# Sample states of a retention layer: key-value products directly behind the query-state products

## The chip, the core and the metric

The kernel runs on one core of a Trainium2 chip. The metric is device microseconds (us) of one execution. A core has engines that run side by side and meet at semaphores: PE (TensorE, matrix products; PEld is its loading of weights), DVE (VectorE), ACT (ScalarE), POOL (GpSimd) and SP (SyncE), which in this kernel issues most of the DMAs. Each engine takes its instructions in order, so one that waits holds up all behind it on the same engine.

## The reference, cut to what matters

The kernel computes one layer of a hybrid decoder for 1024 prompt tokens and for 8 sample sequences of 4 new tokens. The part that the change touches is the retention branch of the samples, with 4 heads, keys of 256 and values of 512 elements, and a state of 256x512 for each sequence and head:

```python
def retention_chunk(q, k, v, s_prev, log_g):
    ...
    intra = jnp.einsum('bhij,bjhe->bihe', scores, v)
    q_decay = jnp.exp((idx[:, None] + 1.0) * log_g[None, :])
    cross = jnp.einsum('bihd,bhde->bihe', q, s_prev) * q_decay[None, :, :, None]
    k_decay = jnp.exp((c - 1.0 - idx)[:, None] * log_g[None, :])
    s_new = (jnp.exp(c * log_g)[None, :, None, None] * s_prev
             + jnp.einsum('bjhd,bjhe->bhde', k * k_decay[None, :, :, None], v))
    return intra + cross, s_new
```

`s_prev` is read from `state_ret` and `s_new` is an output, `ret_sample`. So every state is loaded, multiplied with the queries, scaled, increased by the products of keys and values, and stored.

## The kernel before, in words

The layer is worked off in stages: latents and gates, attention of the samples over their pages, retention, attention of the prompt, and the projections back. Nearly all large products are split in a high and a low part and take three matmuls each (`mac`, L262 to L268); `gemm` (L270) does a projection of 128 columns in three thirds of 352 tokens, with 8 such triples to a third, and takes its weights from `load_w` (L253), which loads them with SP (tile `wr`, L246), rounds them on ACT (`wh`, L247) and takes the rest on DVE (`wl`, L199).

In the retention stage the loop over heads `h` stands at L1055. For each head, `prompt_chunks` goes through the eight chunks of the prompt, and `sample_state` (L965) comes behind its last chunk. Beside both run the projections for the next head (`head_in`, L1050), or, for the last head, the MLA gate projections (`gate_tiles`). The two streams are woven at L1070: each is a Python generator that yields costs, and `woven` (L115) always continues the stream that is less far along in its total cost (27.9 or 32.4 for the first, 50.3 or 31.8 for the other). So a `yield 1.2` in `sample_state` is a place where projections may come in, and its number says how many. The order of the text is then the priority with which the framework's planner orders each engine's instructions. It may depart from it where it takes an operand to be late.

`sample_state` works in four turns `n` per head (L1017), each over half of the rows `i` and half of the key dimension `m`, with four sequences `r`:

- four query-state products into `px` (L1021), 128 rows by 32 columns of the array each, at four column positions, so that they run beside one another. In turns 2 and 3 they are held in the program's order (`keep_in_program_order`, L1024);
- `yield 1.2` (L1025);
- four key-value products into `pd` (L1029), 32 rows by 128 columns each, at four row positions. They take two PSUM banks of `ac` and two of `tr`, of three each; `px` holds the third of `ac` throughout the loop. They read `kxs` and `vst`, which do not depend on the states;
- four updates of the state on DVE (L1031), which read `pd` and overwrite the state in place, and behind every second one a DMA from SP that stores the pair (L1033);
- in turns 0 and 1, two loads of the states of turn `n + 2` (L1035, `states`, L956, issued at L961). There are four buffers `st` of two states each, so such a load waits for the store of the turn two before to be done;
- `yield 2.6` (L1036).

The states of turns 0 and 1 are loaded ahead, from within `prompt_chunks` (L942 and L952).

Of the kernel before, what the change touches and what calls it, by code (L numbers as in the profile page):

```python
# [161 lines left out]
def decode_step(ctx: ExitStack, tc: tile.TileContext, A: dict, O: dict):  # L162
# [17 lines left out]
    def tr():  # L180
        return banks["pool"].tile([P, 512], F32, tag="tr", name="tr", bufs=3)

    def ac():
        return banks["pool"].tile([P, 512], F32, tag="ac", name="ac", bufs=3)
# [7 lines left out]
    def b32(ap):  # L192
        return ap.bitcast(F32)
# [10 lines left out]
    def C(name, i=0, w=None, rows=P):  # L204
        o, ww = at[name]
        w = ww if w is None else w
        return cst[:rows, o + i * w:o + (i + 1) * w]
# [619 lines left out]
    def group_norm(po, n, qd, qd2):  # L827
        st6 = small(p4, "st6", 6, 2)
        dve.bn_stats(out=st6[:n], in_=po)
        mv = small(p4, "mv", 2, 2)  # L830
        dve.bn_aggr(out=mv[:n], in_=st6[:n])
        v = small(p4, "gv", 1, 2)
        dve.tensor_scalar(v[:n], mv[:n, 1:2], qd2, EPS, op0=ALU.mult, op1=ALU.add)
        r = small(p4, "gr", 1, 2)
        pool.tensor_tensor(out=r[:n], in0=v[:n], in1=nhalf[:n], op=ALU.pow)
        s = small(p4, "gs", 1, 2)
        dve.tensor_tensor(out=s[:n], in0=r[:n], in1=qd, op=ALU.mult)
        nb = small(p4, "gb", 1, 2)
        dve.scalar_tensor_tensor(out=nb[:n], in0=mv[:n, 0:1], scalar=-1.0, in1=s[:n], op0=ALU.mult, op1=ALU.mult)  # L839
        on = p4.tile([P, DV], F32, tag="row", name="on", bufs=2)  # L840
        act.activation(on[:n], po, AF.Identity, bias=nb[:n], scale=s[:n])  # L841
        return on

    def gate_in(h, n, cols):
        g = p4.tile([P, 4, P], F32, tag="g", name="g", bufs=3)[:, :, :n]
        sp.dma_start(g, gtD[h][:, :, cols])
        return g

    def gate_out(h, on, n, cols, g):
        pt = tr()  # L850
        for f in range(4):
            pe.transpose(pt[:, f * P:f * P + n], on[:n, f * P:(f + 1) * P], ident[:n, :n])  # L852
        for f in range(4):
            dve.scalar_tensor_tensor(out=g[:, f, :], in0=pt[:, f * P:f * P + n], scalar=gnw[:, 4 * h + f:4 * h + f + 1],
                                     in1=g[:, f, :], op0=ALU.mult, op1=ALU.mult)
        sp.dma_start(goD[h][:, :, cols], g)
# [99 lines left out]
    def states(h, i, m):  # L956

        pairs = []
        for half in range(2):
            st = p4.tile([P, 2, DV], F32, tag="st", name="st", bufs=4)  # L960
            sp.dma_start(st, A["state_ret"][0].rearrange("(r i) h (m p) e -> i m h p r e", i=2, m=2)[i, m, h][:, 2 * half:2 * half + 2])  # L961
            pairs.append(st)
        return pairs

    def sample_state(h, X):  # L965

        q, k = X["qS"], X["kS"]
        g4 = float(np.exp(NS * lg[h]))
        sl = slice(SEQ, NT)
        ks = p4.tile([P, 2, 4, 4, 8], F32, tag="knh", name="ks", bufs=2)  # L970
        for m in range(2):
            pool.tensor_copy(ks[:, m], k[:, m].rearrange("p (r x) -> p r x", x=8).unsqueeze(2).to_broadcast([P, 4, 4, 8]))
        pt = tr()
        for m in range(2):
            pe.transpose(pt[:, m * P:(m + 1) * P], ks[:, m].rearrange("p r c x -> p (r c x)"), ident)
        kt = p4.tile([P, DK], F32, tag="knl", name="kt", bufs=2)
        act.activation(kt, pt[:, :DK], AF.Copy, scale=C("kdS", h, 1))
        ks = p4.tile([P, 2, 2, NR], F32, tag="knh", name="ks2", bufs=2)
        for m in range(2):
            pool.tensor_copy(ks[:, m], k[:, m].unsqueeze(1).to_broadcast([P, 2, NR]))  # L980
        qm = p4.tile([P, 2, 288], F32, tag="row", name="qm", bufs=2)
        pool.memset(qm, 0.0)
        for m in range(2):
            pool.tensor_copy(qm[:, m].rearrange("p (b x) -> p b x", x=36)[:, :, :NS], q[:, m].rearrange("p (b t) -> p b t", t=NS))
        yield 1.0
        ps = ac()
        for n in range(8):
            for part in range(2):
                pe.matmul(ps[:2 * NR], few[:, n, :], X["W"][n][part], start=n + part == 0, stop=n == 7 and part == 1)
            yield 0.45  # L990
        vs = p4.tile([2 * NR, DV], F32, tag="vnl", name="vs", bufs=2)
        act.copy(vs, ps[:2 * NR])
        pss = tr()
        for m in range(2):
            pe.matmul(pss[:2 * NR, :NR], ks[:, m].rearrange("p c x -> p (c x)"), q[:, m], start=m == 0, stop=m == 1)
        sm = p4.tile([2 * NR, NR], F32, tag="sms", name="sms", bufs=1)
        dve.tensor_tensor(out=sm, in0=pss[:2 * NR, :NR], in1=C("maskS", h, NR, 2 * NR), op=ALU.mult)
        yield 1.0
        pt = tr()
        pe.matmul(pt, turn, vs, start=True, stop=True)  # L1000
        vr, vst = (p4.tile([P, DV], F32R, tag="vnh", name=n, bufs=2) for n in ("vr", "vst"))
        dve.tensor_copy(vr, pt)
        dve.scalar_tensor_tensor(out=vst, in0=b32(vr), scalar=C("minus", 1, 1), in1=pt, op0=ALU.mult, op1=ALU.add)
        kr = p4.tile([P, DK], F32R, tag="knl", name="kr", bufs=2)
        dve.tensor_copy(kr, kt)
        dve.scalar_tensor_tensor(out=kt, in0=b32(kr), scalar=C("minus", 0, 1), in1=kt, op0=ALU.mult, op1=ALU.add)
        kxs = []
        for i in range(2):
            kxs.append(p4.tile([P, DK], F32R, tag="knh", name="kx", bufs=2))
            dve.tensor_scalar(kxs[i], kt, C("seq2", i, 1), None, op0=ALU.mult)  # L1010
        yield 1.0
        px = ac()
        g = gate_in(h, NR, sl)
        out = O["ret_sample"][0].rearrange("(r i) h (m p) e -> i m h p r e", i=2, m=2)
        turns = [(i, m) for i in range(2) for m in range(2)]
        loaded = X["st"]
        for n, (i, m) in enumerate(turns):  # L1017
            pairs = loaded.pop(0)
            st = [pairs[r // 2][:, r % 2, :] for r in range(4)]
            for r in range(4):  # L1020
                ins = pe.matmul(px[32 * r:32 * r + 32, :], qm[:, m, 32 * (2 * r + i):32 * (2 * r + i) + 32], st[r],  # L1021
                                start=n == 0, stop=n == 3, tile_position=(0, 32 * r), skip_group_check=True)
                if n > 1:
                    tc.keep_in_program_order(ins)  # L1024
            yield 1.2  # L1025
            pd = [ac(), ac(), tr(), tr()]
            for r in range(4):
                rs = slice(32 * r, 32 * r + 32)
                pe.matmul(pd[r], kxs[i][rs, m * P:(m + 1) * P], vst[rs], start=True, stop=True, tile_position=(32 * r, 0))  # L1029
            for r in range(4):  # L1030
                dve.scalar_tensor_tensor(out=st[r], in0=st[r], scalar=g4, in1=pd[r], op0=ALU.mult, op1=ALU.add)  # L1031
                if r % 2:
                    sp.dma_start(out[i, m, h][:, r - 1:r + 1], pairs[r // 2])  # L1033
            if n < 2:
                loaded.append(states(h, *turns[n + 2]))  # L1035
            yield 2.6  # L1036
        xs = p4.tile([P, DV], F32, tag="row", name="xsb", bufs=2)
        act.copy(xs, px)
        po = ac()
        pe.matmul(po[:NR], sm, vs, start=True, stop=False)  # L1040
        pe.matmul(po[:NR], C("sel"), xs, start=False, stop=True)
        on = group_norm(po[:NR], NR, C("qdS", h, 1, NR), C("qd2S", h, 1, NR))
        yield 1.0
        if h + 1 < HR:
            late.append((h, on, NR, sl, g))
        else:
            gate_out(h, on, NR, sl, g)
            yield 0.5
# [545 lines left out]
```

## Time and profile before

| What | Value |
|---|---|
| Median of 3 runs | 2188.82 us (2184.98 to 2189.14) |
| The profiled execution | 2187.65 us, of which the span of the trace is 2185.8 us |
| PE busy | 2138.7 us |
| DVE busy | 1234.5 us |
| ACT busy | 731.1 us |
| The 16 turns of `sample_state` | 911.8 to 1363.5 us of the span, in four groups, one per head |
| Query-state products (L1021) | 128 matmul records, 605 ns median |
| Key-value products (L1029) | 64 matmul records, 496 and 490 ns median |
| State updates (L1031) | 64, 680 ns median, on DVE |
| State loads within the trace (L961) | 32, 512 KB each, 4.1 us median from issue to landing |
| State stores (L1033) | 32, 512 KB each, 3.7 us median |

The 605 ns are the record of one pass of a product. Four stand beside one another in the array, and a product of plain f32 operands has two passes, so a turn's eight records take about one us. In a timeline, a row gives the start, the duration, the engine, the line and the tiles written and read; in brackets stands the idle time before, with what ended it. Matmuls overlap by design, so the distance from one start to the next tells more of the cost than the durations do.

### The profile page before, as it was taken

To read this page: it belongs to the slowest core of one execution; us is meant where nothing else is said; L and a number is where in the kernel's file an instruction comes from. 1 tells how busy PE (TensorE), PEld (TensorE's weight loads), DVE (VectorE), ACT (ScalarE), POOL (GpSimd) and SP (SyncE) were. 2 spreads that over 40 slices of the span, in tenths; PEclk is the share of its full clock that TensorE was granted. 3 is DMA by queue.
4 is the path that set the end of the run, shared out by engine and by line. 5 is a ranking of instruction groups with operands and counts; after the bars stand their busy time and mean duration, and the time that the engine had idled before them with its cause. 6 is when DMAs were issued, how large, how long until landed. Compare 5 with 4: busy or idle time off the path is not lost.

```text
span 2185.8 us, 38552 instructions
## 1 busy us (share of the span) xinstructions
PE 2138.7 (98%) x15368; PEld 1858.5 (85%) x15368; DVE 1234.5 (56%) x2776; ACT 731.1 (33%) x1537; POOL 317.4 (15%) x511
## 2 busy tenths in 40 slices
PE   8999999999999999999999999899998999999997
PEld 7997877777777898888788887788887999999997
DVE  5424564565655356656666664778676353444465
ACT  6412322333333222221222311454556342222243
POOL 2211111111110022222121220122221000000121
PEclk9999999999999999999999999999999999999999
DMA  8447666566565321532613517110112353234243
GB/s 239 136 139 263 213 218 230 177 250 216 211 231 178 112 68 49 172 116 88 208 41 121 179 52 252 51 37 12 38 51 73 130 197 98 82 96 124 78 143 115
DMA packets 264356, 299.71 MB, mean 137 GB/s; under 512 B 26544, under 2 KB 221744, under 8 KB 260080
## 3 DMA queue, kind: packets, MB, share of 16 engines
q1 hardware_dynamic: 254960, 213.36, 31.5%
q0 software_dynamic: 9216, 83.89, 10.2%
q8 instruction: 121, 1.98, 0.4%
q14 instruction: 59, 0.48, 0.1%
HBM read 233.03 MB, written 64.17 MB: 136 GB/s over the span
## 4 chain that ended last, share of the span: by engine, by line
PE 61%; issue 4%; DVE 3%; DMA 1%; ACT 1%; POOL 1%; POOLq 0%; ACTq 0%; DVEq 0%; SPq 0%
PE mm L266 15%; PE mm L267 14%; PE mm L268 14%; PE ac L266 2%; PE ac L268 2%; PE ac L267 2%; PE mm L1302 2%; PE tr L1288 1%; PE ac L1245 1%; PE sc L652 1%; PE tr L852 1%; PE x L683 1%; PE ac L874 1%; PE ac L1246 1%; PE ac L1247 1%
## 5 line engine op out<-in xcount | busy, mean ns | idle before, releaser
L266 PE MATMUL mm<-xh,wh 128*128 128x352 f32 x1344 | 458.3, 341 | 1.0 <-ACT gev L413 0.8
L267 PE MATMUL mm<-xl,wh 128*128 128x352 f32 x1344 | 436.5, 325 | 0.0
L268 PE MATMUL mm<-xh,wl 128*128 128x352 f32 x1344 | 435.5, 324 | 0.0
L266 PEld LDWEIGHTS mm<-xh,wh 128*128 128x128 f32 x1344 | 253.1, 188 | 104.2 <-issue 86.5
L267 PEld LDWEIGHTS mm<-xl,wh 128*128 128x128 f32 x1344 | 254.3, 189 | 5.0 <-issue 2.7
L268 PEld LDWEIGHTS mm<-xh,wl 128*128 128x128 f32 x1344 | 253.9, 189 | 1.5 <-issue 1.5
L199 DVE TENSOR_TENSOR wl<-wr,wh 128x512 fp32r<-128x512 f32 (+2 forms) x251 | 168.5, 683 | 133.2 <-ACT wh L247 107.0
L247 ACT CAST wh<-wr 128x512 fp32r<-128x512 f32 x216 | 129.7, 618 | 285.0 <-PE mm L267 219.9
L648 DVE STREAM_TRANSPOSE kt<-craw 128x512 f32<-128x512 f32 x256 | 160.6, 681 | 108.3 <-PE sc L652 73.1
L413 ACT ACTIVATE gev<-mm 128x352 f32<-128x352 f32 x120 | 55.6, 464 | 233.0 <-PE mm L268 151.5
L266 PE MATMUL mm<-mh,wh 128*128 128x352 f32 x384 | 124.4, 324 | 1.8 <-DVE M L1417 1.8
L268 PE MATMUL mm<-mh,wl 128*128 128x352 f32 x384 | 124.3, 324 | 0.0
L268 PE MATMUL mm<-gh,wl 128*128 128x352 f32 x384 | 124.3, 324 | 0.0
L266 PE MATMUL mm<-gh,wh 128*128 128x352 f32 x384 | 124.3, 324 | 0.0
L267 PE MATMUL mm<-ml,wh 128*128 128x352 f32 x384 | 124.2, 324 | 0.0
L267 PE MATMUL mm<-gl,wh 128*128 128x352 f32 x384 | 124.1, 323 | 0.0
L266 PE MATMUL mm<-wv,xh 128*128 128x512 f32 x256 | 103.0, 402 | 0.0
L267 PE MATMUL mm<-wv,xh 128*128 128x512 f32 x256 | 100.9, 394 | 0.0
L268 PE MATMUL mm<-wv,xl 128*128 128x512 f32 x256 | 100.7, 393 | 0.0
L841 ACT ACTIVATE on<-ac,gb,gs 128x512 f32<-128x512 f32 (+1 forms) x36 | 28.0, 778 | 208.5 <-DVE gb L839 208.2
L652 PE MATMUL sc<-kt,q 32*32 32x512 f32 x2560 | 91.5, 600 | 0.0
L1523 POOL TENSOR_TENSOR xr<-x1h,x1l 128x352 f32<-128x352 f32 x24 | 24.4, 1039 | 406.2 <-DVE pT L199 326.1
(384 smaller groups left out, 4563.0 us busy)
## 6 DMA issues: line engine op xcount, KB each, us to landing
wr<-in_w_in_dram SPq DMA_DIRECT2D x144, 256.0 KB, 3.0
st<-in_state_ret_dram SPq DMA_DIRECT2D x32, 512.0 KB, 4.1
out_ret_sample_dram<-st SPq DMA_DIRECT2D x32, 512.0 KB, 3.7
wr<-in_w_ple_gate_dram SPq DMA_DIRECT2D x48, 256.0 KB, 2.7
gt<-gev SPq DMA_DIRECT2D x48, 176.0 KB, 1.8
gl<-go SPq DMA_DIRECT2D x16, 528.0 KB, 7.6
gate<-ga SPq DMA_DIRECT2D x16, 528.0 KB, 3.3
g<-gt SPq DMA_DIRECT2D x32, 256.0 KB, 3.1
```

Source lines behind the costliest of these rows:

```text
L199: dve.tensor_tensor(out=out, in0=src, in1=b32(hi), op=ALU.subtract)
L247: hi_by[0](hi, raw)
L266: pe.matmul(out, wh, xh, start=first, stop=False)
L267: pe.matmul(out, wh, xl, start=False, stop=False)
L268: pe.matmul(out, wl, xh, start=False, stop=last)
L413: act.activation(t, ps, func)
L648: dve.transpose(kt[:, 2 * i + s].rearrange("p (n r) -> p n r", r=32), src)
L652: pe.matmul(sc[32 * v:32 * v + 32, q, :], Q["q4"][qs_, j + v // 2, 2 * (g % 2) + v % 2, :], kt[qs_, v, :], start=n == 0, stop=n == NJ // 2 ...
L683: pe.matmul(pv[32 * v:32 * v + 32, :KL], pT[:, n, 32 * v:32 * v + 32], keys[v % 2][:, 8 * (v // 2) + n, :], start=n == 0, stop=n == 7, til ...
L841: act.activation(on[:n], po, AF.Identity, bias=nb[:n], scale=s[:n])
L1302: pe.matmul(po[:, :256], v[a][w], t[:, x, 256 * a:256 * a + 256], start=j + a + part == 0, stop=False, skip_group_check=True)
L1523: pool.tensor_tensor(out=xr, in0=b32(x1[f][0][:, sl]), in1=b32(x1[f][1][:, sl]), op=ALU.add)
```

## The change

The first `yield` of a turn is taken out, and its cost is put on the second one, so that the sum of a turn stays 3.8. The four key-value products, the four updates, the stores and the loads of the state then stand directly behind the four query-state products, and all projections of the turn come behind them.

```diff
@@ -1022,7 +1022,6 @@
                                 start=n == 0, stop=n == 3, tile_position=(0, 32 * r), skip_group_check=True)
                 if n > 1:
                     tc.keep_in_program_order(ins)
-            yield 1.2
             pd = [ac(), ac(), tr(), tr()]
             for r in range(4):
                 rs = slice(32 * r, 32 * r + 32)
@@ -1033,7 +1032,7 @@
                     sp.dma_start(out[i, m, h][:, r - 1:r + 1], pairs[r // 2])
             if n < 2:
                 loaded.append(states(h, *turns[n + 2]))
-            yield 2.6
+            yield 3.8
         xs = p4.tile([P, DV], F32, tag="row", name="xsb", bufs=2)
         act.copy(xs, px)
         po = ac()
```

## The prediction

> **What bounds the kernel now.** I read the page first, then the busy times of the stage that the change touches, then PE's own timeline in it.
>
> ```profile
> span 2185.8 us, 38552 instructions
> PE 2138.7 (98%) x15368; PEld 1858.5 (85%) x15368; DVE 1234.5 (56%) x2776; ACT 731.1 (33%) x1537; POOL 317.4 (15%) x511
> ```
>
> ```profile
> 904.00:945.00 41.00, 40.60 (x242) 32.35 (x242) 26.89 (x49) 11.63 (x24) 9.43 (x10) 1.00 0.66 214
> ```
>
> PE is busy 98% of the span and 40.60 of 41.00 us in the turns of head 0 (the columns are PE, PEld, DVE, ACT, POOL, then the granted clock, 1.00, and the DMA share, 0.66). DVE has a third of this stretch free (26.89 of 41.00). So the time of this stage is PE's work plus the places where PE stands still or changes over. Whatever the change takes from these counts in full; whatever it does on other engines counts only if PE comes to wait for it. The first turn of head 0 on PE:
>
> ```profile
> 911.51 0.32 PE L268 MATMUL mm<-xh,wl 128*128 128x352 f32 x1
> 911.76 1.07 PE L1021 MATMUL ac<-st,qm 128*32 128x512 f32 x8
> 912.76 0.43 PE L266 MATMUL mm<-xh,wh 128*128 128x352 f32 x1
> 913.02 0.32 PE L267 MATMUL mm<-xl,wh 128*128 128x352 f32 x1
> ...
> 914.64 0.32 PE L268 MATMUL mm<-xh,wl 128*128 128x352 f32 x1
> 914.89 0.50 PE L1029 MATMUL ac<-vst,kx 32*128 32x512 f32 x2
> 915.33 0.43 PE L266 MATMUL mm<-xh,wh 128*128 128x352 f32 x1
> 915.59 0.32 PE L267 MATMUL mm<-xl,wh 128*128 128x352 f32 x1
> ```
>
> Read starts, not durations. From 913.02 to 914.64 there are ten projection matmuls, 0.162 us apart. The step into the query-state products (911.51 to 911.76) is 0.25, so 0.09 is lost in it. They hold PE for 1.00 (to 912.76), and the first projection behind them needs 0.26 until the next one, 0.10 too many. The same three steps at the key-value products are 0.25 in, 0.44 for themselves and 0.26 for the first projection behind. So each of the two excursions per turn has about 0.19 of changing over that is visible beside its own work.
>
> **The change, first part: one changeover fewer.** The twelve projections from 912.76 to 914.64 move behind the key-value products. No instruction is added or removed. PE then goes projections, query-state, key-value, projections: one step into a small tile (0.09) and one slow first projection (0.10) go, 0.19 per turn, and the step from one small tile to the other is new. The trace has no such step between just these two, but one like it: the two products that end a head's samples, of 64x32 and of 128x32 of the array.
>
> ```profile
> 1090.99 1.04 PE L1040 MATMUL ac<-vs,sms 64*32 64x512 f32 x2
> 1091.96 1.04 PE L1041 MATMUL ac<-xsb,cst 128*32 128x512 f32 x2
> ```
>
> The second follows 0.97 behind the first, which is no more than the 1.00 from the query-state products to a projection. So I cost the new step at nothing, and the saving at 16 turns x 0.19 = 3.0 us. Bounds: if the new step costs a whole changeover, the saving is 0; below that I see nothing in these rows, since 0.19 is all that any change of shape shows.
>
> ```profile
> 914.89 0.18 PEld L1029 LDWEIGHTS ac<-vst,kx 32*128 32x128 f32 x2 [0.21 <-issue]
> ```
>
> The weights of the key-value products load in 0.18 us (PEld's record). [...]
>
> **Second part: states that come late.** In seven of the eight turns 2 and 3, the query-state products stand still in the middle or come in two parts. The rows, head by head:
>
> ```profile
> 928.00 1.05 PE L1021 MATMUL ac<-st,qm 128*32 128x512 f32 x4
> 929.41 1.05 PE L1021 MATMUL ac<-st,qm 128*32 128x512 f32 x4 [0.36 <-DMA st<-in_state_ret_dram]
> 930.39 0.43 PE L266 MATMUL mm<-xh,wh 128*128 128x352 f32 x1
> ...
> 1071.79 1.05 PE L1021 MATMUL ac<-st,qm 128*32 128x512 f32 x4
> 1073.41 1.05 PE L1021 MATMUL ac<-st,qm 128*32 128x512 f32 x4 [0.57 <-DMA st<-in_state_ret_dram]
> 1074.40 0.43 PE L266 MATMUL mm<-xh,wh 128*128 128x352 f32 x1
> ...
> 1081.53 1.05 PE L1021 MATMUL ac<-st,qm 128*32 128x512 f32 x4
> 1082.87 1.05 PE L1021 MATMUL ac<-st,qm 128*32 128x512 f32 x4 [0.28 <-DMA st<-in_state_ret_dram]
> 1083.85 0.43 PE L266 MATMUL mm<-xh,wh 128*128 128x352 f32 x1
> ...
> 1217.10 1.53 PE L1021 MATMUL ac<-st,qm 128*32 128x512 f32 x8
> 1218.56 0.42 PE L266 MATMUL mm<-xh,wh 128*128 128x352 f32 x1
> ...
> 1225.69 1.37 PE L1021 MATMUL ac<-st,qm 128*32 128x512 f32 x8
> 1226.99 0.43 PE L266 MATMUL mm<-xh,wh 128*128 128x352 f32 x1
> ...
> 1349.77 1.05 PE L1021 MATMUL ac<-st,qm 128*32 128x512 f32 x4
> ...
> 1351.86 1.05 PE L1021 MATMUL ac<-st,qm 128*32 128x512 f32 x4 [0.69 <-DMA st<-in_state_ret_dram]
> 1352.85 0.43 PE L267 MATMUL mm<-xl,wh 128*128 128x352 f32 x1
> ...
> 1358.03 1.05 PE L1021 MATMUL ac<-st,qm 128*32 128x512 f32 x4
> ...
> 1359.85 1.05 PE L1021 MATMUL ac<-st,qm 128*32 128x512 f32 x4
> ...
> 1361.19 0.50 PE L1029 MATMUL ac<-vst,kx 32*128 32x512 f32 x2
> ```
>
> The bracket tells only the idle part; the loss is start to next projection, less the 1.00 of an undisturbed turn. Head 0: 930.39 - 928.00 - 1.00 = 1.39 in turn 2. Head 1: 1.61 and 1.32. Head 2: 0.46 and 0.30. Head 3, turn 2: 3.08 less 1.00 and less 0.26 for the one projection between the pairs, 1.82; turn 3: nothing is late, but the pairs stand apart, and a pair alone holds PE as long as both, so about 1.1 is lost. All together 8.0 us.
>
> Why are they late? The states of turn 2 go into the buffers of turn 0, so their load waits for that turn's store, and the store for its updates. SP's own queue shows it:
>
> ```profile
> 918.74 1.58 SPq L1033 DMA_DIRECT2D out_ret_sample_dram<-st  x2
> ...
> 921.50 1.65 SPq L961 DMA_DIRECT2D st<-in_state_ret_dram  x2
> ```
>
> The chain begins with the key-value products: 914.89 products, 918.74 stores, 921.50 loads, 929.41 landed, 14.5 us. The change starts it where the query-state products end, at 912.76: 2.13 earlier in turn 0, and in turn 1 by 2.61 (923.01 less 920.40):
>
> ```profile
> 920.40 0.43 PE L266 MATMUL mm<-xh,wh 128*128 128x352 f32 x1
> ...
> 923.01 0.50 PE L1029 MATMUL ac<-vst,kx 32*128 32x512 f32 x2
> ```
>
> The products that wait come earlier too, by 0.19 for each turn and by each stall that goes. In head 0 the second pair was 1.41 late; 2.13 - 0.38 - 1.41 leaves 0.34 of margin: the stall goes, 1.4. In head 1, with the same distances, turn 2 was 1.62 late (margin 0.13: 1.6 gone), but turn 3 was 1.34 late and its products now come 1.62 + 0.57 earlier: 2.61 - 1.34 - 2.19 = -0.9, so some 0.9 of wait stays and 0.4 goes. Head 2's 0.46 and 0.30 go. Head 3 weaves in fewer projections (1.2 / 32.4 x 31.8 = 1.2 of cost in the gap, against 1.2 / 27.9 x 50.3 = 2.2), so its shift is some half of 2.13 and under the 2.09 by which its second pair stood apart; I take half of its 2.9: 1.4. Sum: 1.4 + 1.6 + 0.4 + 0.8 + 1.4 = 5.6 us. Bounds: 8.0 if all goes, and 0 if DVE or SP do not pass the earlier start on.
>
> **What is moved with it.** Per turn four updates on DVE, two stores and (turns 0 and 1) two loads on SP move past two us of projections and their evacuation: past ACT's copies and DVE's rotations and `wl` parts, and past `wr` loads in SP's queue. I cost that at nothing. The cover on DVE is its free third; on SP it is that the stores' wait is only moved, not lengthened:
>
> ```profile
> SPq L1033 <- DVE st L1031: 40.8, 32, 4.6
> ```
>
> If that cover were gone, `wr` loads behind a waiting store would be late, and PE would wait for weights. It does not today: of the 0.40 us that PE is idle in the stretch of head 0, 0.36 is the wait for states shown above. One wait could take the place of the old one: the key-value products need the PSUM banks that the last turn's updates read.
>
> ```profile
> 916.56 0.68 DVE L1031 SCALAR_TENSOR_TENSOR st<-st,ac 128x512 f32<-128x512 f32 x1
> ...
> 918.63 1.28 DVE L1031 SCALAR_TENSOR_TENSOR st<-st,tr 128x512 f32<-128x512 f32 x2
> ```
>
> Turn 0's updates end at 919.91 and turn 1's key-value products would start at 920.40. So even updates that came no earlier at all would leave them free by 0.5.
>
> **The sum.** 3.0 + 5.6 = 8.6 us off the profiled execution's 2187.65 us gives 2179.1 us. The median of the runs shown lies 1.2 us higher, so against it 2180.2; I say 2180. All this is 0.4% of the time; a measurement of this kernel can tell about 0.2%, 4.4 us, from no change.
>
> **The rivals.**
>
> *The loads stay late.* The chain from products to landed states has 14.5 us, and most of it is transfers: 512 KB stores and loads at a DMA share of 0.66. If these only queue longer when they start earlier, the stalls stay and the changeovers alone go: 2187.65 - 3.0 = 2184.7. For it: margins of 0.34 and 0.13 us are thin. Against: the chain starts at DVE's updates, and they do start earlier. Chance 0.20.
>
> [...] Chance 0.12.
>
> *Slower: DVE's queue.* Four updates of 0.68 come 2 us sooner, ahead of rotations that free the buffers of ACT's copies, which in turn free PE's two `mm` banks. A bank is filled by 24 matmuls, 3.9 us, and that is the slack: 2.7 of updates and the 1.2 that DVE was already behind (key-value products done at 915.33, first update at 916.56) use all of it. It decides from there: with one more instruction of that size in front, PE waits some 0.7 in each of 12 turns, 8.4 us; less the 3.0 gained this is +5.4: 2193. Against it: DVE's free third. Chance 0.08.
>
> **How the numbers follow.** Forecast 0.60, with 2176.5 (8.0 + 3.0 gone) and 2183 as its own ends. Loads stay late 0.20, nothing gained 0.12, DVE 0.08. Faster by over 0.2% is the forecast, 0.60; the two middle cases and a tenth of the last make within 0.2%, 0.33; slower 0.07. The range takes in the forecast and the two middle cases: 2176 to 2189.
>
> **What would show it.** [...] The first projection behind L1029 comes 1.44 after L1021's start (if it is 1.6, the step costs a changeover). The stores' issue lies some 2 us nearer to the query-state products, and the wait of L1021 for the state loads falls to one turn of head 1 and part of head 3 (else the first rival). PE's waits name DVE or ACT in the stage: the last rival. What would make it all wrong: an order on PE or SP that changes elsewhere in the kernel, which these rows do not show.

## The result, and the profile after

| | before | changed |
|---|---|---|
| Median of 12 runs each, us | 2189.12 (2184.98 to 2196.56) | 2180.82 (2178.55 to 2185.36) |
| Ratio, with its 95% interval | | 0.9971 (0.996 to 0.9981) |
| The profiled execution, us | 2187.65, span 2185.8 | 2184.80, span 2183.0 |

The change makes the kernel faster by 0.29%: 0.0029 x 2189.12 = 6.3 us, with an interval of 4.2 to 8.8 us. (The two medians of the table lie 8.3 us apart; the ratio and its interval are what is used here.) The profiled execution of the changed kernel is one of the slowest of its twelve runs, so the two profiles differ by 2.85 us only. That pair alone would have told half of the gain. All the same it shows where the time goes. The head of its page:

```profile
span 2183.0 us, 38548 instructions
PE 2134.5 (98%) x15368; PEld 1859.5 (85%) x15368; DVE 1240.9 (57%) x2776; ACT 729.6 (33%) x1537; POOL 319.1 (15%) x511
```

The numbers of PE, DVE, ACT and POOL instructions are those of before; only their order is new. PE's timeline of the first turn in the changed kernel (the key-value products are now on L1028, the updates on L1030, the stores on L1032):

```profile
911.79 1.06 PE L1021 MATMUL ac<-st,qm 128*32 128x512 f32 x8
912.78 0.50 PE L1028 MATMUL ac<-vst,kx 32*128 32x512 f32 x2
913.22 0.43 PE L266 MATMUL mm<-xh,wh 128*128 128x352 f32 x1
```

No projection stands between the products any more. The key-value products start 0.99 behind the query-state products, and the first projection starts 1.43 behind them, where 1.44 was forecast for a step that costs nothing and 1.6 for one that costs a changeover.

What became of the late states shows further on in the same timeline: turn 3 of head 0, then turn 2 of head 3.

```profile
935.75 1.05 PE L1021 MATMUL ac<-st,qm 128*32 128x512 f32 x4
937.05 1.05 PE L1021 MATMUL ac<-st,qm 128*32 128x512 f32 x4 [0.25 <-DMA st<-in_state_ret_dram]
938.03 0.50 PE L1028 MATMUL ac<-vst,kx 32*128 32x512 f32 x2
...
1346.58 1.05 PE L1021 MATMUL ac<-st,qm 128*32 128x512 f32 x4
1348.86 1.05 PE L1021 MATMUL ac<-st,qm 128*32 128x512 f32 x4 [1.22 <-DMA st<-in_state_ret_dram]
1349.84 0.50 PE L1028 MATMUL ac<-vst,kx 32*128 32x512 f32 x2
```

The first of these turns lost nothing before and now loses 938.03 - 935.75 - 1.00 = 1.28. The second loses 1349.84 - 1346.58 - 1.00 = 2.26, no less than before. The wait in head 0 that the prediction wanted gone (turn 2, 1.4) is gone, but the stall has moved one turn on.

SP's timeline of head 0 in the changed kernel shows how much of the early start came through:

```profile
917.29 1.58 SPq L1032 DMA_DIRECT2D out_ret_sample_dram<-st  x2
921.18 0.35 SPq L246 DMA_DIRECT2D wr<-in_w_in_dram  x1
921.58 0.94 SPq L961 DMA_DIRECT2D st<-in_state_ret_dram  x2
```

The first store stands at 917.29, against 918.74 before: 1.45 of the 2.13 us arrive there. The first load stands at 921.58, against 921.50: nothing arrives. The second load, which brings the pair that was late, stands directly behind it at 922.06, against 922.78 before: 0.72 arrive. The store is not what holds the first load. The view by line, for this one store alone, gives its time from issue to landing:

```profile
DMA to landing us min/median/max: 2.8/2.8/2.8
```

So it had landed at about 920.1, and its buffer was free 1.5 us before the load was issued. The waits of SP's queue in head 0 (905 to 947 us; in all, times, longest) name what came in between, first before, then after:

```profile
SPq L961 <- DMA out_ret_sample_dram<-st: 5.7, 4, 3.8
SPq L246 <- DVE wl L199: 4.0, 5, 1.4
```

```profile
SPq L246 <- DVE wl L199: 8.2, 7, 2.3
SPq L961 <- DMA out_ret_sample_dram<-st: 4.1, 2, 3.3
```

Before, all four state loads of the head wait for their stores. After, only the two of turn 3 do. Those of turn 2 stand in SP's queue behind the `wr` load at 921.18, which waits 2.3 us until DVE has made a `wl` and so freed the buffer. DVE's timeline shows why that is later than it was, again before and after:

```profile
915.76 0.68 DVE L199 TENSOR_TENSOR wl<-wr,wh 128x512 fp32r<-128x512 f32 x1
...
923.54 1.28 DVE L1031 SCALAR_TENSOR_TENSOR st<-st,ac 128x512 f32<-128x512 f32 x2 [0.69 <-PE ac L1029]
```

```profile
917.18 1.28 DVE L1030 SCALAR_TENSOR_TENSOR st<-st,tr 128x512 f32<-128x512 f32 x2
...
919.69 1.43 DVE L199 TENSOR_TENSOR wl<-wr,wh 128x512 fp32r<-128x512 f32 x1
...
924.33 1.27 DVE L1030 SCALAR_TENSOR_TENSOR st<-st,ac 128x512 f32<-128x512 f32 x2
```

Before, a `wl` stood ahead of turn 0's updates (916.56 to 919.91); the change puts the updates (915.99 to 918.46) ahead of it. And DVE has no pause from 915.78 to 927.40. So the updates of turn 1 start at 924.33, 0.79 later than before, though their products come 2.77 sooner (at 920.24). The other heads with projections of the next head beside them agree: in heads 0 to 2, the first load of turn 2 follows its store by 4.3 to 4.7 us in the three profiles of the changed kernel's order (2.8 to 3.2 in the two of before), and turn 1's updates start 11.9 to 12.5 us behind the head's first L1021 (11.8 before).

What did help turn 3 is that turn 1's stores land sooner: the loads of turn 3, which wait for them alone, follow 3.5 to 5.5 us behind, where they followed by 5.7 to 7.5. Why is not shown. These stores are now issued some 3.6 us behind the second load of turn 2, where it was 1.2 to 2.1, so an overlap that went is likely.

The view by windows shows head 0's four turns (from the first L1021 to the products that end the samples), before and after, in the columns of the prediction with GB/s behind the DMA share:

```profile
911.76:945.66 33.90, 33.54 (x205) 26.57 (x204) 23.07 (x42) 8.92 (x18) 9.33 (x10) 1.00 0.71 237
```

```profile
911.79:945.32 33.53, 33.20 (x205) 26.59 (x205) 24.27 (x42) 8.62 (x18) 7.82 (x8) 1.00 0.76 258
```

**An account by stretch.** One execution of each kernel says little about 6 us: the late turns differ by 1 us and more from one execution to the next of the same program. The table takes all five profiles that there are of the two kernels (three are of runs below; the planner gave *norm_late* the changed kernel's order on every engine). "Turns" adds up the four stretches like the one just shown, one per head; "behind" adds up the three from there to the next head's first L1021, in which the change leaves PE's work as it was; "stalls" is, within the turns, start of a turn's L1021 to the next other instruction behind its last one on PE, less 1.00.

| profile | turns of heads 0 to 3 | sum | behind, sum | stalls |
|---|---|---|---|---|
| before | 33.90, 35.44, 33.26, 26.85 | 129.45 | 323.5 | 8.9 |
| before_again | 34.76, 35.19, 33.98, 26.97 | 130.90 | 323.5 | 10.4 |
| changed | 33.53, 32.48, 32.07, 27.18 | 125.26 | 325.2 | 6.5 |
| after_again | 31.71, 32.36, 32.64, 26.89 | 123.60 | 324.0 | 5.4 |
| norm_late | 31.71, 32.47, 31.71, 27.64 | 123.53 | 323.5 | 5.4 |

The means give 124.13 - 130.18 = -6.05 us in the turns and 324.2 - 323.5 = +0.7 behind them, together -5.3, within the interval of the timing. What lies ahead of the first turn and behind the last one differs by 2 to 3 us between executions of one program and is left out of this account. The 0.7 is a new wait. In the changed kernel's first profile it stands at the end of head 2's prompt projections:

```profile
1229.76 1.04 PE L1039 MATMUL ac<-vs,sms 64*32 64x512 f32 x2
...
1242.92 0.38 PE L882 MATMUL tr<-cst,k 128*128 128x128 f32 x2
1244.56 0.50 PE L266 MATMUL ac<-vnh,smh 128*128 128x512 f32 x1 [1.26 <-ACT vnh L823]
```

PE waits 1.26 us for the next head's first values, which ACT rounds. ACT's timelines show where ACT lost its lead, the kernel before first, then the changed one:

```profile
1229.71 0.45 ACT L790 COPY rx<-mm 128x352 f32<-128x352 f32 x1 [1.16 <-PE mm L268]
...
1234.27 0.45 ACT L790 COPY rx<-mm 128x352 f32<-128x352 f32 x1 [2.81 <-PE mm L268]
...
1240.28 0.77 ACT L841 ACTIVATE on<-ac,gb,gs 32x512 f32<-32x512 f32 x1 [5.55 <-DVE gb L839]
...
1246.48 0.59 ACT L823 CAST vnh<-mm 128x512 fp32r<-128x512 f32 x1 [1.31 <-PE mm L268]
```

```profile
1227.99 0.62 ACT L247 CAST wh<-wr 128x512 fp32r<-128x512 f32 x1 [3.65 <-DMA wr<-in_w_in_dram]
...
1229.52 0.85 ACT L790 COPY rx<-mm 128x352 f32<-128x352 f32 x2
...
1239.17 0.77 ACT L841 ACTIVATE on<-ac,gb,gs 32x512 f32<-32x512 f32 x1 [8.81 <-DVE gb L839]
...
1243.93 0.58 ACT L823 CAST vnh<-mm 128x512 fp32r<-128x512 f32 x1
```

Measure from the products that end the samples (L1040 before, at 1234.12; L1039 after, at 1229.76, 4.36 sooner). Before, the first key copy `rx` came 4.4 ahead of them and the second 0.15 behind. After, both come together 0.24 ahead, because the first stands behind a rounding of weights that waits 3.65 us for its load. The same rounding ran at 1227.44 before, so PE is 4.36 early there and the weights are not. DVE then rotates both thirds one after the other before it gets to the samples' norm, so `on` comes 9.4 behind the products instead of 6.2, and `vnh`, 4.8 behind `on`, is late.

### The profile page after: what moved, and what is told of

Its sections match the earlier page's. It is cut to its first block, busy times and chain, and to the rows that moved or that the text cites. A ratio compares the mean times of both kernels' runs of the same rounds, so it can differ in the third digit from the quotient of the medians.

```text
span 2183.0 us, 38548 instructions
## 1 busy us (share of the span) xinstructions
PE 2134.5 (98%) x15368; PEld 1859.5 (85%) x15368; DVE 1240.9 (57%) x2776; ACT 729.6 (33%) x1537; POOL 319.1 (15%) x511
## 4 chain that ended last, share of the span: by engine, by line
PE 60%; issue 4%; DVE 3%; ACT 1%; POOL 1%; DMA 1%; POOLq 0%; ACTq 0%; SPq 0%; DVEq 0%
PE mm L266 15%; PE mm L268 14%; PE mm L267 14%; PE ac L266 2%; PE ac L268 2%; PE ac L267 2%; PE mm L1301 2%; PE tr L1287 1%; PE sc L652 1%; PE ac L1244 1%; PE x L683 1%; PE tr L852 1%; PE ac L874 1%; DMA wr<-in_w_in_dram 1%; PE ac L1246 1%
```

## The experiments

Every edit is against the changed kernel unless said otherwise. The ratios are to the kernel before, run beside it on the same chip.

| run | median, us | ratio (95%) |
|---|---|---|
| updates_late | 2186.66 | 1.0003 (0.9994 to 1.0012) |
| kv_first | 2190.09 | 1.0019 (1.001 to 1.0029) |
| shifted | 2179.93 | 0.9972 (0.9962 to 0.9982) |
| shifted_mild | 2184.58 | 0.9988 (0.9978 to 0.9998) |
| no_reload | 2178.41 | 0.9964 (0.9951 to 0.9976) |
| no_reload_apart | 2178.19 | 0.996 (0.9945 to 0.9976) |
| norm_late | 2180.24 | 0.9968 (0.9954 to 0.9981) |
| norm_late_mild | 2184.02 | 0.9984 (0.9975 to 0.9994) |
| loads_pool | 2189.42 | 1.0018 (1.0009 to 1.0027) |
| best | 2179.0 | 0.997 (0.9958 to 0.9982) |
| after_again | 2180.36 | 0.9974 (0.9965 to 0.9984) |
| before_again | 2189.28 (one run) | |

**What are the changeovers worth by themselves?** Without the loads of turns 2 and 3, no state can be late. Both kernels were run like that, first the changed one, then the one before:

```diff
-                loaded.append(states(h, *turns[n + 2]))
+                loaded.append(pairs)
```

> As the changed kernel, but turns 2 and 3 load no states: they read those that turns 0 and 1 have updated, so 16 loads of 512 KB and all waits of PE for them are left out. If the stalls cost what the profile shows (6.6 us): 6 to 7 us less than the changed kernel, ratio to before 0.994. If a stall only covers a later wait (weights, PSUM banks): 2 to 4 us less, 0.9955, and PE waits for DVE or ACT instead.

> The kernel before (products apart), with the 16 state loads of turns 2 and 3 left out as in no_reload: those turns read what turns 0 and 1 have updated. Without waits for states, the four turns of a head (first query-state product to the end of the turns) show the changeovers alone: 31.71 us each for heads 0 to 2 and 23.0 us for head 3 with the products together. Changeover theory: 0.19 us for each of four turns more, 32.5 and 23.8 us. If a changeover costs nothing net: 31.7 and 23.0 us. The total says what is given back behind the heads: no_reload gained 11.3 us in the turns over the kernel before and gave back some 4 of it.

The view by windows, head 0's four turns, with the products together and then apart:

```profile
908.68:940.39 31.71, 31.71 (x205) 26.50 (x205) 23.36 (x40) 8.52 (x18) 7.73 (x8) 1.00 0.59 190
```

```profile
910.46:942.96 32.50, 32.50 (x205) 26.43 (x204) 23.55 (x43) 8.60 (x18) 9.35 (x10) 1.00 0.58 190
```

PE stands nowhere still in either, has the same 205 matmul records, and needs 0.79 less: 0.20 for each turn. The other heads give 0.79 (31.71 to 32.50), 0.79 and 0.78 (23.00 to 23.78), so the changeovers are worth 3.15 us. The weights of the key-value products, 0.18 us by PEld's records before and after the change, add nothing to the step that shows: with the products together, 1.00 us lie from the start of the query-state products to that of the key-value products (908.68 to 909.68), and with them apart 1.00 to the first projection (910.46 to 911.46).

Yet the two times are the same. What is gained in the turns goes again behind them: 328.3 against 323.6 us, 4.7. With the products together, PE waits 2.0 us for `vnh` at the end of head 2, and then runs slowly for a while (last section), which makes 3.3 of the 4.7; with them apart it doesn't wait there. Where no state is late, the change is worth nothing that these runs can tell (0.9964 from five runs and 0.996 from four).

**Does it depend on PE's order, or on the place of the updates?** Here the updates, stores and loads are put 1.2 of cost behind the products, where they stood before. The order of PE's instructions is that of the changed kernel.

```diff
                 pe.matmul(pd[r], kxs[i][rs, m * P:(m + 1) * P], vst[rs], ...)
+            yield 1.2
             for r in range(4):
...
-            yield 3.8
+            yield 2.6
```

> The products stand together as in the changed kernel, but the updates, stores and loads of a turn come 1.2 of cost later, where they stood before. Theory A (the gain is changeovers on PE, 0.19 us in each of 16 turns): all of the 3.0 us stay, the stalls of the query-state products on state loads are no shorter than before (8 us or a little less, since the pairs of the last head are no longer apart), ratio to the kernel before 0.9975 to 0.9990. Theory B (the gain is the earlier chain of updates, stores and loads): nothing is left of it, ratio 0.9995 to 1.0005, and PE shows stalls of 8 us or more.

The ratio is 1.0003: no gain at all. Its turns take 126.85 us, still 3.3 less than the mean of before, about the changeovers. Its stalls are 8.7 in all, as many as before's (9.7 on average, with some 1.0 of projections between the parted pairs of head 3 counted in). And 327.4 us behind the turns give 3.9 back: PE waits there 0.7, 0.7 and 1.5 us for `vnh`.

But the run does not part PE's order from the place of the updates, as it was meant to. In the turns that feed the late states, DVE takes the updates where the changed kernel has them. In heads 0 to 2, they start 4.0 to 4.2 us behind the head's first L1021 in turn 0 (changed 3.6 to 4.2, before 4.8 to 4.9) and 11.9 to 12.1 in turn 1 (changed 11.9 to 12.5, before 11.8). And as in the changed kernel, turn 2 of these heads has no stall. The runs differ further on. Turn 2's updates come sooner (18.0 to 18.5 us, changed 20.5 to 22.5), so that their stores follow turn 3's loads by 1.0 us instead of over 3, and turn 3 loses 1.0 to 2.0 in each of the heads 0 to 2. Turn 3's updates come later (30.0 to 31.0, changed 25.7 to 28.3), and end 0.2 us ahead of the products that end the samples, instead of 2.7 or more. So the run shows that the same order on PE is worth nothing with another order on DVE. What PE's order gains with the updates of all turns at their old places stays open.

**Start the chain earlier still?** The key-value products ahead of the query-state products:

```diff
+            pd = [ac(), ac(), tr(), tr()]
+            for r in range(4):
+                rs = slice(32 * r, 32 * r + 32)
+                pe.matmul(pd[r], kxs[i][rs, m * P:(m + 1) * P], vst[rs], ...)
             for r in range(4):
...
-            pd = [ac(), ac(), tr(), tr()]
-            for r in range(4):
-                rs = slice(32 * r, 32 * r + 32)
-                pe.matmul(pd[r], kxs[i][rs, m * P:(m + 1) * P], vst[rs], ...)
```

> As the changed kernel, but within a turn the key-value products stand ahead of the query-state products, so that the products that wait for states start 0.44 us later and the updates still start where both are done. Theory A: the changeovers are the same, each of the five stalls left (6.6 us together) is 0.44 shorter, so 2 us less than the changed kernel, ratio to before 0.996. A rival: the key-value products now come 1.0 us earlier and wait for the PSUM banks of the last turn's updates (they had 0.5 us of margin), so the stall moves and the ratio is 0.997 to 0.998.

It is slower than before, 1.0019. The turns are as short as the changed kernel's (122.95, and 0.44 per head for the products that stand ahead of the first L1021), the stalls 6.1. But the three stretches behind take 332.9 us, 9.4 more than before. Of these, 1.3 are the products that now stand ahead of the next head's L1021 (3 x 0.44), and 4.8 are waits of PE for `vnh` behind each of the heads 0 to 2 (1.3, 1.4 and 2.1), where before has none; some 1.5 more come with the last of them (last section). The other 1.8 stay open. The waits have changed place.

**Is it the time between turns?** More projections behind the first turns and fewer behind the last leave the states more time:

```diff
-            yield 3.8
+            yield (4.6, 4.6, 4.2, 1.8)[n]
```

> As the changed kernel, but the projections are dealt out unevenly over the turns (costs 4.6, 4.6, 4.2, 1.8 in place of four times 3.8), so turns 2 and 3 come 8 to 12 matmuls later (1.5 to 2 us). Theory A with the chain of stores and loads as a fixed length from the updates: the stalls left (6.6 us) fall to about 2 us (those of the last head, 2.3 and 1.9, in part), 4 to 5 us less than the changed kernel, ratio to before 0.995. Rival: the loads are held up by SP's queue and DVE's order, which follow the projections, so the stalls move along and the ratio is that of the changed kernel, 0.997.

The stalls fall to 1.7, so the time between turns is what the late states lack. The time is that of the changed kernel (0.9972 against 0.9971), for a new wait stands in turn 0. PE's timeline, and DVE's in front of it:

```profile
919.52 0.43 PE L268 MATMUL mm<-xh,wl 128*128 128x352 f32 x1 [1.12 <-DVE wl L199]
```

```profile
914.34 1.28 DVE L1030 SCALAR_TENSOR_TENSOR st<-st,ac 128x512 f32<-128x512 f32 x2
915.53 1.28 DVE L1030 SCALAR_TENSOR_TENSOR st<-st,tr 128x512 f32<-128x512 f32 x2
...
918.04 1.42 DVE L199 TENSOR_TENSOR wl<-wr,wh 128x512 fp32r<-128x512 f32 x1
```

PE comes to the next weights before DVE has their low part `wl`, by 1.1, 0.9 and 1.0 us in heads 0 to 2: DVE makes it behind four updates, two of which begin at 914.34. A milder split was to find a place between the two:

```diff
-            yield 3.8
+            yield (3.8, 4.6, 4.4, 2.4)[n]
```

> The changed kernel with costs 3.8, 4.6, 4.4, 2.4 in place of four times 3.8: the first turn as in the changed kernel (so that its weights do not come late, as they did by 1.2 to 1.4 us in each of the first three heads with 4.6 there), turns 2 and 3 later by some 9 and 18 matmuls. Theory A and C: stalls on states 2 to 3 us (last head), no late weights, nothing given back behind the heads: turns of the four heads together 120 to 121 us, stretches behind them as in the kernel before, ratio 0.9950 to 0.9960. Rival: the late weights move to turn 1 (51 projections there), ratio as with the stronger shift, 0.997.

It is worse than either, 0.9988. The stalls are 2.4, but now PE waits for the high part `wh` in a later turn, by 0.2, 1.5 and 0.5 us in heads 0 to 2, and head 1's turns take 35.40 us in its profile, where the changed kernel has 32.4 to 32.5. Part of that is a stretch of 3.1 us behind the wait of 1.5 in which projections start 0.29 us apart instead of 0.16 (last section).

**Is ACT's wait at the norm the cause behind the heads?** The last step of the samples' norm was put off to where its result is used:

```diff
-        on = p4.tile([P, DV], F32, tag="row", name="on", bufs=2)
-        act.activation(on[:n], po, AF.Identity, bias=nb[:n], scale=s[:n])
-        return on
+        def out():
+            on = p4.tile([P, DV], F32, tag="row", name="on", bufs=2)
+            act.activation(on[:n], po, AF.Identity, bias=nb[:n], scale=s[:n])
+            return on
+        return out if later else out()
```

> The changed kernel, but the normalisation of a head's sample rows on ACT is issued where its transposes are (behind the next head's first values) in heads 0 to 2, so that ACT no longer waits 9 us for it ahead of the copies of the last rotated keys. Theory C (what the turns gain is given back behind a head, where PE waits for the next head's first values, held up on ACT and DVE by the last rotations): the stretch behind head 2 falls from 105.3 us to 103.8 us, the others stay at 109.9, ratio to before 0.9960 to 0.9968. Rival (DVE alone is the bound there, its 2.7 us of updates per turn have pushed the rotations back): the wait of PE for those values stays at 1.3 us or more, ratio 0.997.

> Both of the last two edits in one kernel. If they act on the same wait behind the heads, no better than the better of the two (0.995 to 0.996); if on two, 1 to 2 us better than either.

This failed as an experiment: the planner put every instruction of *norm_late* where it stood in the changed kernel, so `on` is not later and the question is open. The run is a third measurement of the changed kernel: its `vnh` wait is absent, and it has no other time (0.9968). So that wait scatters between 0 and 1.3 us. *norm_late_mild*, the same with the milder split, repeats that split's 0.9988 with 0.9984.

**Is SP's queue what holds the loads?** In SP's rows above, a `wr` load stands directly ahead of the state loads. Here the state loads of turns 2 and 3 are issued by POOL:

```diff
-            sp.dma_start(st, A["state_ret"][0]...)
+            (by or sp).dma_start(st, A["state_ret"][0]...)
...
-                loaded.append(states(h, *turns[n + 2]))
+                loaded.append(states(h, *turns[n + 2], by=pool))
```

> The changed kernel with the state loads of turns 2 and 3 issued from POOL in place of SP. If SP's queue holds the loads up (in the changed kernel the first stores of a head are issued 1.5 to 2.3 us sooner than before, the loads behind them only 0 to 1.2 us, since a weight load that waits for DVE stands between): the loads of turn 2 are issued 1 us sooner or more, and stalls are 1 to 2 us less in all. The price: POOL waits for the stores ahead of the key rotations, so the stretches behind the heads grow; if that is more than the gain, the ratio is 0.998 or above. If SP's queue does not matter: stalls as in the changed kernel, 5 to 6.5 us.

POOL's timeline in head 0:

```profile
922.02 1.60 POOL L961 DMA_DIRECT2D st<-in_state_ret_dram  x2
...
932.06 0.73 POOL L961 DMA_DIRECT2D st<-in_state_ret_dram  x1 [5.78 <-DMA out_ret_sample_dram<-st]
```

The loads of turn 3 wait 5.78 us for the store to land, with nothing else in front of them: that is the chain's own wait, not the queue's. Those of turn 2 come behind POOL's rotations, at 922.02, no sooner than from SP (and 912.29, the first L1021 of this run, is 0.5 later). The kernel is slower (1.0018, stalls 10.6, of which 5.3 in turn 2 of head 3). So SP's queue is not what holds turn 3's loads. For turn 2's this run only put one queue in place of another; that SP's queue holds them in the changed kernel shows in its own rows, further up.

**Is there a better version?** The put-off norm (without effect, as above) with the split of *shifted* in the last head only, whose stalls nothing else had touched:

```diff
-            yield 3.8
+            yield 3.8 if h + 1 < HR else (4.6, 4.6, 4.2, 1.8)[n]
```

> norm_late with the uneven costs (4.6, 4.6, 4.2, 1.8) in the last head alone, where the weights are not those that came late and where most of the stalls that are left stand (2.6 and 2.0 us of 5.3). Expected: heads 0 to 2 and the stretches behind them as in norm_late, the last head's turns 24.7 us in place of 27.6, 3 us less than norm_late and 5 us less than the changed kernel's profile; ratio to before 0.9950 to 0.9958. Rival: the time comes back behind the last head, ratio that of norm_late, 0.9968.

> The changed kernel once more, unedited, for a second profile and beside the others on one chip. Expected: ratio 0.996 to 0.998 as on record. Changeovers as in the first profile (each turn of heads 0 to 2 without stalls 0.79 us less per head). If the stalls of heads 0 to 2 (1.3, 0.8, 0.3 us) and the 1.6 us behind head 2 are fixed by the kernel's order, they return to within 0.3 us; if they hang on how the transfers of one execution fall, they differ by more, and the profiled execution on record (2184.8 us, 4 above the median) was an unlucky one.

> The kernel before once more, unedited, for a second profile. Expected: stalls and parted pairs of 8 to 9 us together as in the first, nothing lost behind the heads; the spread of the sum between the two profiles shows what a difference between two single profiles can mean.

On the same chip the changed kernel has 0.9974 and this one 0.997: the intervals overlap nearly whole, so no gain over the changed kernel is shown. Its last head takes 25.69 us instead of 26.9 to 27.6 in its one profile, which would be 1.2 to 2 us.

The two repeats tell how far one profile can be trusted. Turn 3 of heads 0 to 2 lost 1.3, 0.8 and 0.3 us in the changed kernel's first profile, and 0, 0.6 and 0.9 in *after_again*: these stalls hang on the execution. The kernel before has stalls of 8.9 and 10.4. The times agree better: the three runs of the changed kernel's order have ratios of 0.9971, 0.9974 and 0.9968.

## Why the prediction was right, point by point

- **The sum** was 8.6 us and 2180 us; 6.3 (4.2 to 8.8) and 2180.82 were measured. Sign, main causes and range held; the sum was some 2.3 too large. That the median came within 1 us of the forecast is partly luck: the ratio gives less than the medians do, and one term of the sum was twice what came. The range of 2176 to 2189 also took in the two cases of loads that stay late and of no gain, so that it held says little.
- **Changeovers**, 3.0: 3.15 from the pair without reloads, with no loss at the step between the two small tiles. This term is settled. Per turn, 0.20 was measured where the rows of before gave 0.19. A whole changeover at the new step, which would have left nothing of this term, is shown by no run: the step took 0.99 us in the changed kernel and 1.00 in *no_reload*, as much as from the query-state products to a projection before (1.00).
- **Late states**, 5.6: this is the term that was mis-sized. The turns gained 6.05, of which 3.15 are changeovers; 2.9 are left, and the stalls agree (8.7 without the projections, 5.8 after). As forecast, turn 2 of heads 0 to 2 has no stall in any of the three profiles of the changed kernel. But turn 3 of heads 0 to 2 still loses up to 1.3, by the execution, and head 3 keeps 3.9 to 4.6 us of stalls. The prediction passed the early start of the products in full through the whole chain. In head 0, of 2.13 us in turn 0, 1.45 came to the first store, none to the first load and 0.72 to the second; in turn 1, DVE starts the updates no sooner at all. The rival that the loads stay late was half true, but for another reason than transfers that queue: the loads stood behind a `wr` load that waited for DVE.
- **Moved updates at nothing**: this is where the late states lost their half. The cover that the prediction named, DVE's free third, is real on average, but DVE has no pause for 11.6 us from turn 0 to turn 1 of head 0; and on SP, the moved updates lengthen the wait of a weight load for `wl`. Besides, 0.7 us on average were given back at the next head's first values, and up to 4.7 where no state is late. The cover is missing there too: at the end of a head, the key rotations and the samples' norm stand in a row and PE comes sooner. The rival of DVE's queue named the right kind of wait, but put it at the `mm` banks in each turn, and there no profile of the changed kernel has it.
- **That PE's new order or the moved updates do it** was left together in the sum, and the runs do not part them. The changeovers on PE are shown by themselves within the turns (3.15), but behind the turns they come back in full where nothing else is late. *updates_late* did not put the updates of turns 0 and 1 back.

What stays open: why the weight load ahead of the key copies isn't earlier when PE is, since the one run meant to part this chain changed no order; and how the 2.9 of the states divide between loads that go out sooner and transfers that land sooner.

## What to carry to other kernels

A change that makes PE earlier at one place pays only as far as all chains that feed PE behind it have slack: look for the next product that reads what another engine makes, and measure that engine's lead there before and after (here 0.7 us on average, and 4.7 in *no_reload*, were lost again behind the turns). Moving the start of a long chain of update, store and load is not worth the whole shift: every queue on the way can take up part of it (here 2.13 us at the products were 1.45 at the first store and none at the first load), so look at each one for what stands directly ahead of the moved instruction, and for what the moved instruction now stands ahead of. Where a gain is a few us and the waits depend on transfers, take several profiles of the same program before a difference between two of them is read (here one turn lost 1.28 us in one profile of the changed kernel and nothing in the next).

## What the runs showed of the hardware that was not expected

**PE ran slowly behind some of its short stops.** In *kv_first* PE stood still for 2.13 us ahead of one product; the view by windows from there:

```profile
1246.00:1249.50 3.50, 3.50 (x9) 2.74 (x10) 2.85 (x9) 0.53 (x2) 0.02 (x1) 0.53 0.39 94
1249.50:1253.00 3.50, 3.50 (x16) 2.82 (x16) 1.01 (x3) 1.85 (x3) 1.55 (x3) 0.99 0.30 75
```

The granted clock is 0.53 for 3.5 us and then 0.99, and nine matmuls are done where sixteen follow in the same time. The same came in *no_reload* behind 1.95 us of waiting, at 0.51. It didn't come in the changed kernel behind its 1.26 us. At 0.43 from start to start instead of 0.23, the wait cost 1.5 us more than its own length in *kv_first* and 1.4 in *no_reload*, against the same matmuls in the changed kernel. In these profiles the length of the stop alone does not decide it. In *shifted_mild* a stop of 1.50 us (ahead of 1081.89) was followed by projections 0.29 us apart instead of 0.16 (1083.22 to 1086.28), while in the kernel before a stop of 1.82 us (ahead of 1684.72) was followed by 3.5 us at a clock of 1.00, and in the changed kernel one of 1.65 us (ahead of 1682.00) too. Both kernels have a stop of 2.96 us some 50 us behind the last turns (ahead of 1413.70 before and of 1410.92 after), and the clock over the 3.5 us behind it was 0.68 before and 0.57 after. So stops of 1.50 to 2.96 us were followed by slower matmuls, and not each time.

**Equal programs wait differently.** The three profiles of the changed kernel's order have turns of 125.26, 123.60 and 123.53 us, and the wait for `vnh` is 1.3, 0.2 and 0, with no difference in their instructions' order.
